# Merge gates of an encoder block as block products of seven, on one Trainium2 core

## The chip, the cores and the metric

The kernel runs on one core of a Trainium2 chip. TensorE (PE) does the matmuls and transposes, VectorE (DVE), ScalarE (ACT) and GpSimd (POOL) the elementwise work, and SyncE (SP) sends nearly all DMAs from one queue, in order. The metric is the device time of one execution in microseconds; less is better.

## The reference, cut to what matters

`x` is 1024 tokens by 1024 channels. All projections share one normalised input:

```python
h = rms_norm(x, g_pre[layer])
a_qkv, bq, bk, bv, mq, ga, gb, gm, mg = jnp.split(h @ w_in[layer], split_at, axis=-1)
...                       # oa: dilated window attention in 3 groups, with rotary positions
...                       # ob: grouped-query attention, om: cross-attention into a memory
ya = (oa * jax.nn.silu(ga)) @ w_br_a[layer]
yb = (ob * jax.nn.silu(gb)) @ w_br_b[layer]
ym = (om * jax.nn.silu(gm)) @ w_br_m[layer]
gates = jax.nn.sigmoid((mg + b_merge[layer]).astype(jnp.float32)).astype(dt).reshape(b, s, N_BRANCHES, d)
merged = gates[:, :, 0] * ya + gates[:, :, 1] * yb + gates[:, :, 2] * ym
out = merged @ w_out[layer]
x = x + rms_norm(out, g_post[layer])
```

`mg`, the pre-activation of the merge gates, is a 1024 x 1024 by 1024 x 3072 product. It is what the change computes in another way.

## The kernel before

Operands of the big products are split into a high and a low part (`split`: an ACT copy that rounds, then a DVE subtraction), and a product is made of three matmuls, high by high, high by low and low by high. Tokens stand as `hh[k]`, `hl[k]`, eight tiles of 128 channels x 1024 tokens each. A dense *unit* (`load_w`, `dense`) projects all tokens to 128 output channels: one 512 KB weight load, one split, and for each token half 8 channel tiles x 3 terms = 24 matmuls of 128x512, 48 in all. `mg` has 24 such units, numbered j = 8 i + f for branch i and output tile f.

The program runs in stages. Keys and values of the grouped-query attention and the memory projections come first, then cross-attention, then the grouped-query stage (`b_att`), then the dilated attention (pool `aa`, twelve items (p, g)), then the merge, then the output projection. In the attention stages `weave` interleaves dense units from a queue with the attention's own steps, in proportion to costs that are written in the code; PE's order is the order of recording throughout. A unit's result leaves PSUM by `evac`. `add_gate` makes SiLU gates and stores them to `g2d`; `add_filler` does a merge-gate unit early: times `rb` (the token's scale), tanh, stored to `thd`. `FILL_B = (13, 7, 6, 5, 4, 15, 14)` are filled into the grouped-query stage, beside nine SiLU gates, and `FILL_A = (3, 11, 12)` into the last dilated item.

In the grouped-query stage the steps are counted by n, one per key block. `row_max` is a matmul and a DVE minimum of 512 scores (into `bn`); after eight of them `bnm` is formed, `shift` transposes it and DVE writes it into `QL`; `scores` is two matmuls, the second of which reads `QL`, and an ACT exponential into `bp`; POOL adds the `bp` tiles into `bl`; `pv` is the value product, eight fp32 matmuls, and `final` a sum of `bl`. `LAG_S`, `LAG_T`, `LAG_P`, `LAG_F` (9, 10, 12, 13) say how many n each step trails.

In the merge, `mg_unit` computes one of the 14 units that are left (or loads a filled one), and `y_unit`, two units behind, makes a branch product: 24 matmuls of the gated branch output (`gh`, `gl`) with `w_br`, then DVE's (tanh + 1) times the product and a POOL addition into `accs[f]`. Outputs of the branches come back from `od`, gates from `g2d`, and for branch 1 reciprocal sums from `rld`. The order on ACT, DVE, POOL and SP is left to a scheduler here. Then `wout` is loaded and split, and eight token tiles are projected, normalised and stored.

Of the kernel before, what the change touches and what calls it, by code (L numbers as in the profile page):

```python
# [14 lines left out]
D = 1024  # L15
# [35 lines left out]
def block(ctx: ExitStack, tc: tile.TileContext, x, xT, memT, cst, msk, bcst, tabA, gpost,  # L51
# [179 lines left out]
    wgd = dram.tile([4, 2, 3, S], F32, name="wgd")  # L231

# [410 lines left out]
    with tc.tile_pool(name="ba", bufs=1, reuse_waits="tile") as ba:  # L643
# [31 lines left out]

        def b_att():
            st = {}

            def row_max(i, x):
# [6 lines left out]
                PE.matmul(s, QH[:, kv * 4 + j], KS[:, kv, c * 512:c * 512 + 512], start=True, stop=True)  # L686
                V.tensor_reduce(st[i]["n"][:, j, c:c + 1], s, axis=AX.X, op=OP.min)  # L687
                if x == 7:
                    V.tensor_tensor(nmt[i % 2][:, 64:68], st[i]["n"][:, :, 0], st[i]["n"][:, :, 1], op=OP.min)
# [107 lines left out]
    cbp, cb = pool("cb", "right")  # L797
    with tc.tile_pool(name="aa", bufs=1, reuse_waits="tile") as aa:
# [22 lines left out]
        def rope_half(o, half, p, scale, g):  # L821

            t = slice(half * 512, half * 512 + 512)
            t1 = aa.tile([P, 512], F32, name="t1a", bufs=3)
            t2 = aa.tile([P, 512], F32, name="t2a", bufs=3)
# [253 lines left out]
        def combine(p_, ogs):  # L1079
# [4 lines left out]
            def load(g):  # L1084
                wgt[g] = (aa if p_ < 3 else cb).tile([P, S], F32, name="wgt", bufs=3 if p_ < 3 else 1)
# [40 lines left out]

        todo = []
# [6 lines left out]
        for n in range(len(seq)):  # L1134
            if n + 2 < len(seq):
                add_a(*seq[n + 2])
            elif n + 2 == len(seq):
                for j in FILL_A:
                    add_filler(j)
            last = n + 1 == len(seq)  # L1140
            pieces = plan(items[n], items[n - 1] if n else None, items[n + 1])
            if last:
                pieces += plan(None, items[n], None)
            weave(len(FILL_A) if last else 3, run(pieces), sum(c for _, c in pieces), 1.0)

    end_psum()
# [3 lines left out]
    with tc.tile_pool(name="mg", bufs=1, reuse_waits="tile") as mg:  # L1150
        accs = [None] * 8
        extra.extend((mg, wp))

        def mg_unit(i, f):
            th = mg.tile([P, S], F32, name="th", bufs=3)
            if 8 * i + f in spilled:
                nc.sync.dma_start(th, thd[8 * i + f])
                return th
            w = load_w(wu[U_M + 8 * i + f])
            s = pss()  # L1160
            for half in range(2):
                for _ in dense(w, half, s[:, half]):
                    pass
            V.tensor_tensor(th, s.rearrange("p a b -> p (a b)"), rb, op=OP.mult)
            A.activation(th, th, AF.Tanh, scale=0.5, bias=hbm[:, 8 * i + f:8 * i + f + 1])
            return th

        def y_unit(n, i, f, th, gh, gl):
            wh, wl = load_w(wbr[i, f], 512)
            s = pss()  # L1170
            for half in range(2):
                t = slice(half * 512, half * 512 + 512)
                terms = []
                for k in range(4):
                    terms += [(wh[:, k, :], gh[k][:, t]), (wh[:, k, :], gl[k][:, t]), (wl[:, k, :], gh[k][:, t])]
                passes(s[:, half], terms)
            sv = s.rearrange("p a b -> p (a b)")
            if n == 0:
                accs[f] = mg.tile([P, S], F32, name=f"acc{f}")
                V.scalar_tensor_tensor(accs[f], th, 1.0, sv, op0=OP.add, op1=OP.mult)  # L1180
            else:
                V.scalar_tensor_tensor(th, th, 1.0, sv, op0=OP.add, op1=OP.mult)  # L1182
                G.tensor_tensor(accs[f], accs[f], th, op=OP.add)  # L1183

        def g_load(i):
            ots = []
            for k in range(4):
                ot = (pre or mg).tile([P, S], F32, name="ot", bufs=4 if pre else 2)
                nc.sync.dma_start(ot, od[i, k])
                gt = mg.tile([P, S], F32, name="gt", tag="wr", bufs=2)  # L1190
                nc.sync.dma_start(gt, g2d[i, k])
                V.scalar_tensor_tensor(ot, ot, 0.5, gt, op0=OP.mult, op1=OP.mult)
                if i == 1:
                    gt = mg.tile([P, S], F32, name="gt", tag="wr", bufs=2)
                    for h in range(2):
                        nc.sync.dma_start(gt[h * 64:h * 64 + 64], rld[2 * k + h:2 * k + h + 1].to_broadcast([64, S]))
                    V.tensor_tensor(ot, ot, gt, op=OP.mult)
                ots.append(ot)
            return ots

        def g_split(ots):
            gh, gl = [], []
            for k, ot in enumerate(ots):
                a = mg.tile([P, S], R, name=f"gh{k}")
                b = mg.tile([P, S], R, name=f"gl{k}")
                split(a, b, ot)
                gh.append(a)
                gl.append(b)
            return gh, gl

        def g_prep(i):
            gh, gl = [], []
            for k in range(4):
                ot = mg.tile([P, S], F32, name="ot", bufs=2)
                nc.sync.dma_start(ot, od[i, k])
                gt = mg.tile([P, S], F32, name="gt", tag="wr", bufs=2)
                nc.sync.dma_start(gt, g2d[i, k])
                V.scalar_tensor_tensor(ot, ot, 0.5, gt, op0=OP.mult, op1=OP.mult)
                a = mg.tile([P, S], R, name=f"gh{k}")
                b = mg.tile([P, S], R, name=f"gl{k}")  # L1220
                split(a, b, ot)
                gh.append(a)
                gl.append(b)
            return gh, gl

        pre = None
        steps = [(n, i, f) for n, i in enumerate((2, 1, 0)) for f in range(8)]
        ths = {}
        for m in range(len(steps) + 2):
            if m < len(steps):  # L1230
                n, i, f = steps[m]
                ths[m] = mg_unit(i, f)
            if m >= 2:
                n, i, f = steps[m - 2]
                if f == 0:
                    if n == 0:
                        gg = g_prep(i)
                        for step in combine(3, [OG.pop((3, x)) for x in range(3)]):
                            step()
                        close(cbp)  # L1240
                        prep, pre = pool("pre", "right")
                    else:
                        gg = g_split(ots)
                if f == G_AT and n < 2:
                    ots = g_load(1 - n)
                y_unit(n, i, f, ths.pop(m - 2), *gg)

        close(prep)
        fo = ctx.enter_context(tc.tile_pool(name="fo", bufs=1, side="right", reuse_waits="tile"))
        gp = fo.tile([P, D], F32, name="gp")  # L1250
        nc.sync.dma_start(gp, gpost)
        wo = []
        for k in range(8):
            raw = wp.tile([P, 1024], F32, name="wr", bufs=WR)
            nc.sync.dma_start(raw, wout[k])
            a = hp.tile([P, D], R, name=f"woh{k}", tag="big")
            b = hp.tile([P, D], R, name=f"wol{k}", tag="big")
            split(a, b, raw)
            wo.append((a, b))
        for T in range(NT):  # L1260
            t = slice(T * 128, T * 128 + 128)
            ah = wp.tile([P, 8, 128], R, name="wh")
            al = wp.tile([P, 8, 128], R, name="wl")
            for k in range(8):
                A.activation(ah[:, k], accs[k][:, t], AF.Copy, scale=0.5)
                V.scalar_tensor_tensor(al[:, k], accs[k][:, t], 0.5, ah[:, k].bitcast(F32), op0=OP.mult, op1=OP.subtract)
            sv = pss().rearrange("p a b -> p (a b)")
            cuts = [(0, 512), (512, 1024)] if T < NT - 1 else [(0, 512), (512, 768), (768, 1024)]
            terms = []
            for a, b in cuts:  # L1270
                c = slice(a, b)
                terms.append([])
                for k in range(8):
                    terms[-1] += [(ah[:, k], wo[k][0][:, c]), (ah[:, k], wo[k][1][:, c]), (al[:, k], wo[k][0][:, c])]
# [153 lines left out]
```

## Time and profile before

| what | value |
|---|---|
| median of 3 runs | 1502.12 us (1501.77 to 1502.21) |
| profiled execution, its own time | 1502.03 us |
| its span, first to last instruction | 1500.2 us |
| mean granted TensorE clock | 0.997 |
| PE idle in the span | 26.0 us (1500.2 - 1474.2) |
| grouped-query value products | first at 249.22 us, last at 553.85 us |
| DMA | 119.77 MB, 80 GB/s on average |

Busy times count an instruction from start to modelled end; matmuls overlap, so PE's pace is read from the number of matmuls in a window, not from the length of one. A line such as L687 names a line of the program as printed above. `<-` after the idle time names what ended it.

### The profile page before, as it was taken

To read this page: it belongs to the slowest core of one execution; us is meant where nothing else is said; L and a number is where in the kernel's file an instruction comes from. 1 tells how busy PE (TensorE), PEld (TensorE's weight loads), DVE (VectorE), ACT (ScalarE), POOL (GpSimd) and SP (SyncE) were. 2 spreads that over 40 slices of the span, in tenths; PEclk is the share of its full clock that TensorE was granted. 3 is DMA by queue.
4 is the path that set the end of the run, shared out by engine and by line. 5 is a ranking of instruction groups with operands and counts; after the bars stand their busy time and mean duration, and the time that the engine had idled before them with its cause. 6 is when DMAs were issued, how large, how long until landed. Compare 5 with 4: busy or idle time off the path is not lost.

```text
span 1500.2 us, 20621 instructions
## 1 busy us (share of the span) xinstructions
PE 1474.2 (98%) x7844; PEld 1185.7 (79%) x7844; DVE 838.9 (56%) x1514; ACT 576.4 (38%) x1307; POOL 444.7 (30%) x357
## 2 busy tenths in 40 slices
PE   7999989999999999999999999999999999999998
PEld 7899977667766668888888888888887888888787
DVE  7756466666555435664566567556526442525743
ACT  6543344444444341453444434343443112122321
POOL 1425413444444452321232223123200000223322
PEclk9999999999999999999999999999999999999999
DMA  6332011111211112111121121112136531623432
GB/s 241 103 99 71 30 49 60 56 61 43 64 57 50 56 60 89 43 30 43 45 72 57 43 73 44 43 44 72 57 102 189 176 99 43 216 64 113 137 102 99
DMA packets 55042, 119.77 MB, mean 80 GB/s; under 512 B 13792, under 2 KB 23712, under 8 KB 54816
## 3 DMA queue, kind: packets, MB, share of 16 engines
q1 hardware_dynamic: 54800, 118.34, 25.2%
q8 instruction: 61, 1.00, 0.3%
q14 instruction: 37, 0.30, 0.1%
q10 hardware_dynamic: 144, 0.13, 0.0%
HBM read 96.06 MB, written 22.38 MB: 79 GB/s over the span
## 4 chain that ended last, share of the span: by engine, by line
PE 88%; DVE 5%; DMA 2%; ACT 2%; issue 2%; POOL 1%; SPq 0%; POOLq 0%; DVEq 0%; ACTq 0%
PE d L143 14%; PE d L147 14%; PE d L145 14%; PE sc L125 7%; PE ov L720 4%; PE sc L1282 4%; PE sc L147 3%; PE sc L143 3%; PE sc L145 3%; PE tr L981 3%; PE s L918 2%; PE s L705 2%; PE s L704 2%; PE tr L686 2%; PE d L533 2%
## 5 line engine op out<-in xcount | busy, mean ns | idle before, releaser
L143 PE MATMUL d<-hh,wh 128*128 128x512 f32 x992 | 396.4, 400 | 1.8 <-DVE fth L222 1.8
L147 PE MATMUL d<-hh,wl 128*128 128x512 f32 x992 | 397.4, 401 | 0.0
L145 PE MATMUL d<-hl,wh 128*128 128x512 f32 x992 | 393.3, 397 | 0.0
L105 ACT ACTIVATE wh<-wr 128x1024 fp32r<-128x1024 f32 (+1 forms) x100 | 95.4, 955 | 354.9 <-PE d L145 162.7
L143 PEld LDWEIGHTS d<-hh,wh 128*128 128x128 f32 x992 | 187.1, 189 | 47.1 <-issue 5.0
L145 PEld LDWEIGHTS d<-hl,wh 128*128 128x128 f32 x992 | 186.9, 188 | 42.7 <-issue 5.7
L147 PEld LDWEIGHTS d<-hh,wl 128*128 128x128 f32 x992 | 187.0, 188 | 42.1 <-issue 4.7
L711 POOL TENSOR_TENSOR bl<-bl,bp 128x512 f32<-128x512 f32 x96 | 128.6, 1340 | 142.0 <-ACT bp L707 137.3
L106 DVE TENSOR_TENSOR wl<-wr,wh 128x1024 fp32r<-128x1024 f32 (+1 forms) x100 | 113.7, 1138 | 24.9 <-ACT wh L105 24.7
L687 DVE TENSOR_REDUCE bn<-tr 128x1 f32<-128x512 f32 x128 | 87.6, 689 | 63.6 <-PE tr L686 62.3
L707 ACT ACTIVATE bp<-s 128x512 f32<-128x512 f32 x128 | 75.3, 595 | 84.7 <-PE s L705 84.4
L1183 POOL TENSOR_TENSOR acc<-acc,th 128x1024 f32<-128x1024 f32 x16 | 45.4, 2839 | 202.5 <-DVE th L1182 202.5
L837 POOL TENSOR_TENSOR aq<-t1a,t2a 128x512 f32<-128x512 f32 x24 | 54.5, 2272 | 163.6 <-DVE t1a L831 157.5
L831 DVE SCALAR_TENSOR_TENSOR t2a<-d,tab 32x512 f32<-32x512 f32 x96 | 65.9, 687 | 62.7 <-PE d L147 57.8
L837 POOL TENSOR_TENSOR ak<-t1a,t2a 128x512 f32<-128x512 f32 x24 | 55.1, 2297 | 118.3 <-DVE t1a L830 118.3
L147 PE MATMUL sc<-hh,wl 128*128 128x512 f32 x224 | 87.3, 390 | 1.7 <-DVE wl L106 1.7
L143 PE MATMUL sc<-hh,wh 128*128 128x512 f32 x224 | 87.3, 390 | 0.0
L145 PE MATMUL sc<-hl,wh 128*128 128x512 f32 x224 | 87.2, 389 | 0.0
L830 DVE TENSOR_TENSOR t2a<-d,tab 32x512 f32<-32x512 f32 x96 | 65.9, 687 | 23.5 <-PE d L147 22.1
L930 DVE CUSTOM_DVE_ANT_0 pra<-s,mask 128x192 f32<-128x192 f32 (+2 forms) x192 | 56.7, 349 | 36.3 <-PE s L918 24.5
L125 PE MATMUL sc<-gh,wh 128*128 128x512 f32 x192 | 74.7, 389 | 0.0
L125 PE MATMUL sc<-gl,wh 128*128 128x512 f32 x192 | 74.7, 389 | 0.0
(263 smaller groups left out, 2716.4 us busy)
## 6 DMA issues: line engine op xcount, KB each, us to landing
wr<-in_wu SPq DMA_DIRECT2D x76, 512.0 KB
g2d<-fth SPq DMA_DIRECT2D x24, 256.0 KB
wgt<-wgd SPq DMA_DIRECT2D x24, 256.0 KB
ot<-od SPq DMA_DIRECT2D x12, 512.0 KB
gt<-g2d SPq DMA_DIRECT2D x12, 512.0 KB
wr<-in_wbr SPq DMA_DIRECT2D x24, 256.0 KB
thd<-fth SPq DMA_DIRECT2D x20, 256.0 KB
th<-thd SPq DMA_DIRECT2D x10, 512.0 KB
```

Source lines behind the costliest of these rows:

```text
L105: A.activation(dst_h, src, AF.Copy)
L106: V.tensor_tensor(dst_l, src, dst_h.bitcast(F32), op=OP.subtract)
L125: PE.matmul(out_ps, a, b, start=i == 0, stop=i == n - 1)
L143: PE.matmul(dst, wh[:, k, :], hh[k][:, t], start=k == 0, stop=False)
L145: PE.matmul(dst, wh[:, k, :], hl[k][:, t], start=False, stop=False)
L147: PE.matmul(dst, wl[:, k, :], hh[k][:, t], start=False, stop=k == 7)
L687: V.tensor_reduce(st[i]["n"][:, j, c:c + 1], s, axis=AX.X, op=OP.min)
L707: A.activation(pp, s, AF.Exp, scale=-1.0)
L711: G.tensor_tensor(lsum[i % 2], lsum[i % 2], pp, op=OP.add)
L830: return V.tensor_tensor(out, x, y, op=OP.mult)
L831: return V.scalar_tensor_tensor(out, x, scale, y, op0=OP.mult, op1=OP.mult)
L837: G.tensor_tensor(half_of(o, half, g), classes(t1, g), classes(t2, g), op=OP.add)
```

## The change

Two merge-gate units are taken as one pair. With the pair's weights cut into four blocks of 512 channels by 128 outputs (A11, A12 of the first unit, A21, A22 of the second) and the tokens into four blocks of 512 channels by 512 tokens (B11, B12, B21, B22), the four result blocks are made from seven block products instead of eight, by the Winograd form of Strassen's scheme. A block product is 4 channel tiles x 3 terms = 12 matmuls. Sums of weight blocks (S1 to S4) are made on POOL, for each pair; sums of token blocks (T1 to T4) once, on DVE in the grouped-query stage, split and stored to DRAM in `tsd`, and loaded again for the merge. T4 is loaded over the upper token half of `hh[0..3]`, `hl[0..3]`. Result sums are made on DVE from PSUM, and the tanh goes to `thd` for all units.

22 units become 11 pairs; two are still whole, as fillers of the grouped-query stage. Three SiLU gates move from that stage to the last dilated item. In the pairs and in the branch products that follow them, the queues of ACT, DVE, POOL and SP are in the order of recording (`manual_schedule`). Branch products run after all pairs; their gated operands are written over `hh` and `hl`; output weights are loaded and split during the last eight of them.

```diff
+    tsd = dram.tile([4, 4, 2, P, 512], F32, name="tsd")
...
+        def token_block(k):
+            tb = [ba.tile([P, 512], F32, name=f"tb{j}", bufs=1) for j in range(4)]
...
+            def store(j, src):
+                def fn():
+                    h = ba.tile([P, 512], R, name="tbh", bufs=2)
+                    l = ba.tile([P, 512], R, name="tbl", bufs=2)
+                    split(h, l, src)
+                    for x, part in enumerate((h, l)):
+                        nc.sync.dma_start(tsd[j, k, x], part.bitcast(F32))
+                return fn
+            b11, b12, b22, b21 = tb
+            return [whole(b12, k, 1), whole(b11, k, 0), sub(b11, b12, b11), store(0, b11),
+                    whole(b22, k + 4, 1), sub(b12, b22, b12), store(2, b12),
+                    sub(b22, b22, b11), store(1, b22), whole(b21, k + 4, 0), sub(b21, b21, b22), store(3, b21)]
...
                     row_max(i, x)
+                    if n in (14, 38, 62, 86):
+                        blocks += token_block((n - 14) // 24)
+                    if blocks and n % 2 == 0:
+                        with tc.issue_after(fp["last"].ins):
+                            blocks.pop(0)()
                     yield 216
...
-                if (i, p_) not in ((2, 0), (2, 1), (2, 2)):
+                if (i, p_) not in ((2, 0), (2, 1), (2, 2)) + GATES_A:
...
-                for j in FILL_A:
-                    add_filler(j)
+                for j in GATES_A:
+                    add_gate(*j)
+                early[len(queue)] = first_blocks
...
+                load_block("T2")
+                load_block("T3")
...
+    manual = tc.manual_schedule(engines={ET.Activation, ET.DVE, ET.Pool, ET.SP})
...
+    PRODUCTS = (("A11", "B11"), ("A12", "B21"), ("S2", "T2"), ("S3", "T3"), ("A22", "T4"), ("S4", "B22"), ("S1", "T1"))
...
+    def prod(n, i):
+        an, bn = PRODUCTS[i]
+        dst = pss1()
+        ah, al = [v.rearrange("p (k f) -> p k f", k=4) for v in BL[n][an]]
+        passes(dst, [t for k in range(4) for t in (
+            (ah[:, k], TB[bn][k][0]), (ah[:, k], TB[bn][k][1]), (al[:, k], TB[bn][k][0]))])
+        return dst
...
+    def gate_out(n, u, t, x, z):
+        r = sr.tile([P, 512], F32, name="rs", bufs=2)
+        j = pairs[n][u]
+        add(r, x, z)
+        V.tensor_tensor(r, r, rb[:, half[t]], op=OP.mult)
+        return lambda: (A.activation(r, r, AF.Tanh, scale=0.5, bias=hbm[:, j:j + 1]),
+                        nc.sync.dma_start(thd[j, :, half[t]], r))
...
+    load_block("T3", (2, 3))
+    for j in (1, 2, 3, 4):
+        weight_sum(0, j)
+    load_block("T4")
+    load_pair(1, 0)
+    load_pair(1, 1)
+    load_block("T1")
+    before = None
+    for n in range(len(pairs)):
+        for i in range(7):
+            ps_ = prod(n, i)
+            then = evac(*before) if before else None
+            slot(n, i)
+            if then:
+                then()
+            before = (n, i, ps_)
+    evac(*before)()
...
+    th_load(0)
+    yp = None
+    for m, (n, i, f) in enumerate(steps):
+        s = y_unit(m)
+        if yp:
+            y_evac(*yp)
+        yp = m, s
+        th_load(m + 1)
+        y_load(m + 2)
+        y_split(m + 1)
+        if n < 2:
+            j = 1 - n
+            for what, at in ((g_split, 2), (g_mult, 1), (g_load, 0)):
+                if f - at in (0, 1, 3, 4):
+                    what(j, (0, 1, 0, 2, 3)[f - at], *([slice(0, S)] if at == 2 else []))
+            if j == 1 and f in (0, 1, 3, 4):
+                r_load((0, 1, 0, 2, 3)[f])
+        if m >= 15 and m < 23:
+            wo_load(m - 15)
+        if n == 2:
+            split(*wo[f], raws[f])
...
-START_PAD, END_PAD = 250, 300
+START_PAD, END_PAD = 700, 300
...
-FILL_B = (13, 7, 6, 5, 4, 15, 14)
-FILL_A = (3, 11, 12)
+FILL_B = (16, 17)
+GATES_A = ((0, 1), (0, 2), (0, 3))
```

`slot(n, i)` spreads the preparation over the seven products of a pair: the splits of A22, S4 and S1 in the first three, the next pair's sums and splits in the middle ones, its loads at i = 1 and, two pairs ahead, at i = 6, and the rest of the dilated attention's combination and the first gated operands where they fall due. `evac` handles the product before: P1 is copied by ACT; running sums `v`, `y`, `w` are kept on DVE; four blocks per pair go through `gate_out`. In the branch products, `g_load` fetches a branch output (`ot`) and its gate (`gt`), `r_load` the reciprocal sums (`rt`), `g_mult` multiplies them, `g_split` splits them into `hh` and `hl`; `gt` and `rt` have one buffer each.

More of the change, by code (lines that the diff above doesn't have):

```diff
@@ L1143, in block @@
                 pieces += plan(None, items[n], None)
-            weave(len(FILL_A) if last else 3, run(pieces), sum(c for _, c in pieces), 1.0)
+            weave(len(GATES_A) if last else 3, run(pieces), sum(c for _, c in pieces), 1.0)
+    end_psum()
+    phase_psum("ps_w", s1=6)
+    manual = tc.manual_schedule(engines={ET.Activation, ET.DVE, ET.Pool, ET.SP})
+    manual.__enter__()
+    lo, hi = half
+    srp, sr = pool("sr")
+    t1p, t1l = pool("t1")
+    SF = [sr.tile([P, 512], F32, name=f"sf{j}") for j in range(4)]
@@ new lines, in part, with weight_sum, block_of @@
+    def part(n, j):
+        return BL[n][j // 2][:, half[j % 2]]
+    def weight_sum(n, j):
+        u, v, op = {1: (part(n, 2), part(n, 3), OP.add), 2: (SF[0], part(n, 0), OP.subtract),
+                    3: (part(n, 0), part(n, 2), OP.subtract), 4: (part(n, 1), SF[1], OP.subtract)}[j]
+        G.tensor_tensor(SF[j - 1], u, v, op=op)
+    def block_of(n, nm):
+        src = part(n, 3) if nm == "A22" else SF[int(nm[1]) - 1]
+        t = sr.tile([P, 2, 512], R, name="ch", bufs=5)
+        split(t[:, 0], t[:, 1], src)
+        BL[n][nm] = t[:, 0], t[:, 1]
@@ new lines, in prod, with add @@
+    def prod(n, i):
[5 more added lines that the diff above has]
+        return dst
+    p1, v, y, w = [sr.tile([P, 512], F32, name=f"sp{j}") for j in range(4)]
+    def add(dst, x, z):
+        V.tensor_tensor(dst, x, z, op=OP.add)
+    def gate_out(n, u, t, x, z):
[5 more added lines that the diff above has]
+                        nc.sync.dma_start(thd[j, :, half[t]], r))
@@ new lines, in evac @@
+    def evac(n, i, ps_):
+        if i == 0:
+            A.activation(p1, ps_, AF.Copy)
+        elif i == 1:
+            return gate_out(n, 0, 0, ps_, p1)
+        elif i == 2:
+            add(v, ps_, p1)
+        elif i == 3:
+            add(y, ps_, v)
+        elif i == 4:
+            return gate_out(n, 1, 0, ps_, y)
+        elif i == 5:
+            add(w, ps_, v)
+        else:
+            outs = gate_out(n, 1, 1, ps_, y), gate_out(n, 0, 1, ps_, w)
+            return lambda: [f() for f in outs]
@@ new lines, in block, with th_load, wo_load @@
+    mgp, mg = pool("mg")
+    myp, my = pool("my")
+    accs = [None] * 8
+    wo = [(hh[k + 4], hl[k + 4]) for k in range(4)]
+    wo += [(mg.tile([P, D], R, name=f"woh{k}"), mg.tile([P, D], R, name=f"wol{k}")) for k in range(4, 8)]
+    raws, THS = {}, {}
+    def th_load(m):
+        if m < len(steps):
+            _, i, f = steps[m]
+            THS[m] = my.tile([P, S], F32, name="th", bufs=3)
+            nc.sync.dma_start(THS[m], thd[8 * i + f])
+    def wo_load(k):
+        raws[k] = my.tile([P, D], F32, name="raw", bufs=2)
+        nc.sync.dma_start(raws[k], wout[k])
@@ new lines, in y_unit, with y_evac @@
+    def y_unit(m):
+        n, i, f = steps[m]
+        wh, wl = YW.pop(m)
+        s = pss()
+        for h in half:
+            terms = []
+            for k in range(4):
+                gh, gl = [x[k + 4 * (i == 1)][:, h] for x in (hh, hl)]
+                terms += [(wh[:, k], gh), (wh[:, k], gl), (wl[:, k], gh)]
+            passes(s[:, int(h.start > 0)], terms)
+        return s
+    def y_evac(m, s):
+        n, i, f = steps[m]
+        sv = s.rearrange("p a b -> p (a b)")
+        th = THS.pop(m)
+        if n == 0:
+            accs[f] = mg.tile([P, S], F32, name=f"acc{f}")
+            V.scalar_tensor_tensor(accs[f], th, 1.0, sv, op0=OP.add, op1=OP.mult)
+        else:
+            V.scalar_tensor_tensor(th, th, 1.0, sv, op0=OP.add, op1=OP.mult)
+            G.tensor_tensor(accs[f], accs[f], th, op=OP.add)
```

333 lines of the change are left out of this document (183 added, 150 removed).

## The prediction

> **What bounds the kernel now.** I read the busy summary first, then the chain, then stage windows, then the groups of the grouped-query stage, then single places of the timeline.
>
> ```profile
> PE 1474.2 (98%) x7844; PEld 1185.7 (79%) x7844; DVE 838.9 (56%) x1514; ACT 576.4 (38%) x1307; POOL 444.7 (30%) x357
> PE 88%; DVE 5%; DMA 2%; ACT 2%; issue 2%; POOL 1%; SPq 0%; POOLq 0%; DVEq 0%; ACTq 0%
> ```
>
> PE is busy for all but 26 us of the 1500.2 us span, and the chain that ended last is PE for 88%. So a matmul removed is time removed, as long as PE is still fed. The windows (length, then busy us and count for PE, PEld, DVE, ACT, POOL, then clock, DMA share, GB/s) show the pace and the few holes:
>
> ```profile
> 0.00:20.00 20.00, 13.65 (x99) 13.36 (x100) 12.20 (x19) 14.64 (x21) 0.19 (x4) 1.00 0.93 328
> 210.00:220.00 10.00, 7.50 (x30) 6.12 (x31) 5.81 (x10) 3.07 (x9) 2.42 (x3) 0.66 0.16 54
> 1120.00:1130.00 10.00, 10.00 (x45) 8.26 (x45) 4.03 (x10) 3.29 (x5) 0.00 (x0) 1.00 0.84 286
> 1150.00:1160.00 10.00, 8.31 (x37) 6.56 (x35) 5.63 (x3) 2.73 (x3) 2.39 (x1) 1.00 0.49 133
> 1200.00:1300.00 100.00, 100.00 (x442) 82.79 (x442) 41.80 (x39) 21.10 (x23) 4.45 (x2) 1.00 0.36 109
> 1410.00:1420.00 10.00, 8.73 (x38) 6.57 (x37) 6.28 (x15) 5.23 (x14) 4.09 (x3) 1.00 0.19 56
> ```
>
> 1200 to 1300 is pure merge work: 442 matmuls in 100 us, 0.2263 us each, whatever the 0.39 us that one is drawn long. 1150 to 1160 loses 1.7 us at the start of the merge, 1410 to 1420 loses 1.3 us before the output projection. At 210 to 220 PE had gaps and then ran at a granted clock of 0.66. The groups of 240 to 540 us, the grouped-query stage (busy us and mean ns, then idle time before), and two lines of its timeline (start, length):
>
> ```profile
> L687 DVE TENSOR_REDUCE bn<-tr 128x1 f32<-128x512 f32 x115 | 79.2, 690 | 63.2 <-PE tr L686 62.0
> L106 DVE TENSOR_TENSOR wl<-wr,wh 128x1024 fp32r<-128x1024 f32 x14 | 18.8, 1340 | 0.6 <-ACT wh L105 0.5
> L689 DVE TENSOR_TENSOR bnm<-bn 128x4 f32<-128x4 f32 x15 | 7.7, 515 | 0.4
> L711 POOL TENSOR_TENSOR bl<-bl,bp 128x512 f32<-128x512 f32 x90 | 120.1, 1335 | 134.3 <-ACT bp L707 130.0 <-DVE fth L220 0.9
> 387.13 4.06 POOL L711 TENSOR_TENSOR bl<-bl,bp 128x512 f32<-128x512 f32 x3 [0.19 <-ACT bp L707]
> 387.83 0.61 DVE L689 TENSOR_TENSOR bnm<-bn 128x4 f32<-128x4 f32 x1
> ```
>
> bnm has four columns and takes 0.14 us at its shortest, 0.515 on average. The last two lines say why: it starts inside a POOL addition and ends at 388.44, where the first of POOL's three (1.30 us) ends. A DVE operation with both inputs in SBUF waits here for POOL, 0.37 us on average.
>
> **The matmuls.** Before, 24 merge-gate units of 48 matmuls: 1152. After, two whole units (96) and 11 pairs of 7 products of 12 (924): 1020. The instruction lists of the two built programs agree: 7204 and 7072 matmuls and transposes, 132 fewer. New and old are the same 128x512 form, so 132 x 0.2263 = **29.9 us off**. Nothing else on PE changes in number.
>
> **Steady merge.** Per pair PE needs 84 x 0.2263 = 19.0 us. DVE gets 11 additions and products and 5 splits of 512 columns (16 x 0.69) and one split of 1024 (1.22): 12.3 us; ACT one copy, four tanh, five and one splits, 0.6 + 4 x 0.72 + 5 x 0.63 + 1.06 = 7.7; POOL four sums of 1.34, 5.4. Everything fits under PE, and six banks let PE run up to six products ahead. I cost it at nothing; if DVE lost its cover, the excess over 19.0 would count eleven times. SP's loads go out two to four products ahead of use.
>
> **Moved units.** The grouped-query stage goes from 16 whole units to 8 (6 gates, 2 fillers); three gates take the place of three fillers in the last dilated item, an even trade but for one 0.69 us DVE product per half, under idle DVE. The 8 units' 87 us leave a stage where they were cover. Per group of 8 key blocks PE's list now holds 8 maxima, 16 score matmuls, 2 of the sum and some 22 dense, 48 x 0.2263, plus 3.58 for the value product: 14.5 us, against some 20.5 us between value products in the trace.
>
> **Token sums in that stage.** Forty-eight DVE operations (16 sums, 16 differences, 16 split remainders), four per group in twelve groups, all with two SBUF inputs, 16 ACT copies and 32 stores of 256 KB on SP. DVE per group before them: 8 maxima 5.5, QL 0.69, obt 0.68, bll 0.74, bnm 0.5, half a query preparation 0.69, dense evictions 1.85: 10.7 us. The new ones add 4 x 0.69 = 2.8, and 4 x 0.37 of waits for POOL: 15.0 in all, just over PE's 14.5. What PE waits for is QL: by the lists it has 15 matmuls and a transpose, 3.5 us, from a group's eighth maximum to the score that needs QL (4.4 where a query preparation lies between). DVE there has the maximum, a gate product or a further maximum, bnm, another maximum, one token operation and QL: 5 x 0.69 + 0.14 = 3.6, two waits of 0.37, and about 0.5 for the token operation that it is still in: 4.8. That is 1.3 us late without a query preparation, 0.4 with one, and some 0.2 more for the maxima queued behind it: **1.0 us per group, 12 us in all**. Bounds: with no wait for POOL 4 us; with half a POOL addition (0.67) at each of the three, 20, and if the whole DVE excess shows, 26. I take 12 since bnm's measured mean is the nearest row.
>
> **Start of the merge.** After the last value product SP sends the rest of T3 (1 MB), T4 (2 MB, over `hh` and `hl`), the next pair (1 MB) and T1 (2 MB): 6.29e6 bytes, behind the last gate's store. The two densest windows moved 286 and 328 GB/s; in the middle 20.5 us, with 2.5 us for issue and landing 23 us. The seventh product needs the last quarter of T1 at 6.75 x 2.72 = 18.4 us: **4.6 us late** (3.3 to 6.1). POOL's first sums and S2, S3 are made before this. PE's gaps there can lower the clock: after waits of 2.60 and 1.55 us around 210 us PE ran 6.5 us at 0.50, 3.2 us lost. The new gaps are split by T1's quarters, about 1.2 us each, so I take half, **1.5 us** (0 to 3.2). [...] The 1.7 us lost at 1150 us goes.
>
> **Start of the branch products.** `th_load(0)` stands on SP behind the last tanh store, 4 us into the first unit; then 2.75 MB follow until `rt` of the first tile is there, about 15.5 us. (In the trace `rld` loads issued at 1194.39 were waited for until 1199.25.) DVE takes `g_mult` in hand order ahead of the eviction and of the weight split that the fourth unit needs at 16.3 us: done at about 20, **4 us late** (0 if the loads run ahead, 8 if the single `gt` and `rt` buffers repeat it). Output weights are split during the last eight units, so the 1.3 us before the projection goes.
>
> **Sum** on the profiled run's own 1502.0 (span 1500.2 and 1.8 around it, 0.1 from the median): 1502.0 - 29.9 - 1.7 - 1.3 + 12 + 4.6 + 1.5 + 4 = **1491.2 us**. All low bounds give 1476.4 (4 + 3.3 + 0 + 0 added back), all high ones 1512.4 (26 + 6.1 + 3.2 + 8).
>
> **Rivals.**
> *The covers hold.* From 230 to 240 us DVE was busy 9.15 of 10 us while PE lost only 0.3; if token operations fall into the value products, where DVE has nothing to do, the low bounds apply: 1476.4 us. Against it: they are queued behind maxima, not in that gap. Chance 0.22.
> *POOL and DVE block each other in the grouped-query stage* and it ends slower. POOL's 9.4 us of additions per group must fit into a group of 14.5 us instead of 20.5, so a token operation meets one more often; it decides from 1.9 us per group, when 12 x 1.9 = 23 eats what is left. At a wait of 0.9 us instead of 0.37 at each of the three (wol, split beside POOL's `acc` additions, went from 1.2 to 3.4 us at worst), a group loses 2.5 us, 30 us: 1509 us. Against it: bll, in the same stage, mostly took its bare 0.69. Chance 0.22. [...]
> *The saving isn't delivered*: seven products with hand-ordered queues leave PE waiting for evictions, 2.5 us in each pair: 1502 + 27.5 - 32.9 + 5 = 1502. The 12.3 of 19.0 us speaks against it. Chance 0.06.
>
> **How the numbers follow.** The forecast case has 0.50 and spans 1480 to 1499. Low and high tails beyond 1474 and 1510 are about one in ten each. A measurement of this kernel can tell 0.2%, 3.0 us, from no change. Faster: the forecast but its upper edge, 0.48, and the first rival, 0.22, 0.70; within: 0.07; slower: 0.23.
>
> **What would show it.** Right: 132 fewer matmuls at 0.226 us; PE waits on QL's line of about 1 us per group in the twelve groups with token lines and not in the others; one wait on T1 in the first pair; a wait on a weight split early in the branch products. Wrong: DVE or POOL as the releaser through the pairs, waits on QL under 0.3 or over 2 us per group, or no PE wait at the start of either part.

## The result, and the profile after

The changed kernel takes 1516.29 us (median of 5 runs, 1511.99 to 1517.31), the kernel before beside it 1502.21 us: a ratio of 1.0082 (of the means, as all ratios below), 95% interval 1.0061 to 1.0103. It is slower by 0.8%, and lies above the whole range of the forecast. The profiled execution took 1515.56 us (span 1513.8). First its busy summary and the shares of the chain that ended last:

```profile
PE 1461.9 (97%) x7712; PEld 1164.2 (77%) x7712; DVE 990.3 (65%) x1701; ACT 614.0 (41%) x1396; POOL 521.0 (34%) x401
PE 72%; DVE 12%; DMA 5%; issue 4%; ACT 3%; POOL 3%; SPq 1%; DVEq 0%; POOLq 0%; ACTq 0%
```

PE has its 132 matmuls less, and idles for 51.9 us instead of 26.0; DVE, DMA, ACT and POOL now hold 23% of the chain, where they held 10%. The stretches that the forecast named (length, then busy us and count for PE, PEld, DVE, ACT, POOL, then clock, DMA share, GB/s):

```profile
1070.00:1080.00 10.00, 7.52 (x21) 5.49 (x22) 6.86 (x8) 3.73 (x6) 6.59 (x4) 0.66 0.70 243
1100.00:1120.00 20.00, 17.39 (x69) 13.58 (x68) 18.33 (x19) 7.15 (x11) 7.58 (x4) 0.91 0.49 144
...
1200.00:1250.00 50.00, 50.00 (x222) 41.42 (x221) 34.28 (x45) 18.55 (x29) 12.80 (x8) 1.00 0.51 171
1300.00:1310.00 10.00, 6.80 (x27) 4.71 (x27) 6.98 (x7) 3.04 (x4) 0.00 (x0) 1.00 1.01 315
1410.00:1420.00 10.00, 10.00 (x46) 8.29 (x45) 9.72 (x9) 3.63 (x9) 6.08 (x2) 1.00 0.41 134
```

Steady pairs are what was forecast: 222 matmuls in 50 us, PE without a gap, DVE busy for two thirds. The gap before the projection (1410 to 1420) is gone. The losses are at the start of the pairs, in the third pair and at the start of the branch products. The groups of 240 to 540 us, the grouped-query stage, on DVE and POOL:

```profile
L684 DVE TENSOR_TENSOR tb<-hh,hl 128x512 f32<-128x512 f32 x16 | 20.7, 1291 | 0.0
L106 DVE TENSOR_TENSOR tbl<-tb,tbh 128x512 fp32r<-128x512 f32 x16 | 17.0, 1063 | 0.1
L687 DVE TENSOR_TENSOR tb<-tb,tb 128x512 f32<-128x512 f32 x16 | 15.2, 947 | 0.2
...
L717 DVE TENSOR_TENSOR bnm<-bn 128x4 f32<-128x4 f32 x15 | 7.0, 465 | 0.3
...
L739 POOL TENSOR_TENSOR bl<-bl,bp 128x512 f32<-128x512 f32 x96 | 134.2, 1398 | 83.4 <-ACT bp L735 78.3
```

The 48 token operations last 1.10 us on average ((20.7 + 17.0 + 15.2) / 48), 0.41 over their bare 0.69: the wait for POOL that the forecast took from bnm (0.37). And what PE waited for in the stage (total, times, longest):

```profile
PE s L733 <- DVE QL L723: 7.6, 8, 1.8
PE tr L714 <- DVE bn L715: 4.0, 5, 0.9
PE tr L722 <- DVE bnm L717: 1.5, 3, 1.1
```

QL leads, then the maxima queued behind it. In the twelve groups with token operations, PE waited on QL for 1.20, 1.52, 0.22, 0.82, 1.76 and 1.52 us in the six without a query preparation, and not at all in the six with one.

These waits don't add up to what the stage loses. All PE waits there come to some 16 us; the half clock after the longest one (381.8 to 385.2) costs 1.7 more; and a part can't be seen as idle time at all, because the trace draws a dense matmul 0.39 us long where one starts each 0.2263, so a wait of up to 0.16 us behind it looks busy. Losses below are therefore taken from start times. The whole account, with 0.2263 us a matmul. The first dilated score started at 602.3 us before and at 537.5 after; with eight units (86.9 us) less it was due at 515.4, so the grouped-query stage loses **22.1 us**. The dilated stage takes 517.2 us, as it did. From the first pair's first matmul (1054.7) to the first branch matmul (1279.5) are 224.8 us where eleven pairs need 209.1: **15.7 lost**. From there to the projection (1420.0) 140.5 us where 24 products need 130.4: **10.1 lost**. (The wait of 2.5 us right before the first branch matmul is counted in the 15.7, though it belongs to the branch products. By pairs, the 15.7 are 7.2 in the first, 4.9 in the third, 0.7 in the fourth and 2.7 in the last, with that wait.) The merge before lost 2.6, and the projection is 1.9 shorter. -29.9 + 22.1 + 15.7 + 10.1 - 2.6 - 1.9 = +13.5; the spans differ by 13.6.

### The profile page after: what moved, and what is told of

It reads as the page before. It is cut to its first block, busy times and chain, and to the rows that moved or that the text cites. A ratio compares the mean times of both kernels' runs of the same rounds, so it can differ in the third digit from the quotient of the medians.

```text
span 1513.8 us, 21012 instructions
## 1 busy us (share of the span) xinstructions
PE 1461.9 (97%) x7712; PEld 1164.2 (77%) x7712; DVE 990.3 (65%) x1701; ACT 614.0 (41%) x1396; POOL 521.0 (34%) x401
## 4 chain that ended last, share of the span: by engine, by line
PE 72%; DVE 12%; DMA 5%; issue 4%; ACT 3%; POOL 3%; SPq 1%; DVEq 0%; POOLq 0%; ACTq 0%
PE d L143 12%; PE d L147 12%; PE d L145 12%; PE sc L125 7%; PE s L125 5%; PE sc L1499 4%; PE ov L748 4%; PE tr L1015 3%; DVE bn L715 2%; PE s L952 2%; DMA thd<-rs 2%; DVE tb L684 1%; DMA wr<-in_wbr 1%; POOL sf L1243 1%; PE s L733 1%
## 5 line engine op out<-in xcount | busy, mean ns | idle before, releaser
L143 PE MATMUL d<-hh,wh 128*128 128x512 f32 x864 | 345.9, 400 | 1.8 <-DVE fth L222 1.8
L147 PE MATMUL d<-hh,wl 128*128 128x512 f32 x864 | 347.2, 402 | 0.1
L145 PE MATMUL d<-hl,wh 128*128 128x512 f32 x864 | 342.7, 397 | 0.0
L143 PEld LDWEIGHTS d<-hh,wh 128*128 128x128 f32 x864 | 163.0, 189 | 43.5 <-issue 8.2
L147 PEld LDWEIGHTS d<-hh,wl 128*128 128x128 f32 x864 | 162.9, 189 | 36.4 <-issue 5.3
L125 PE MATMUL sc<-hh,wh 128*128 128x512 f32 x384 | 121.9, 398 | 7.6 <-ACT wh L105 5.1
L106 DVE TENSOR_TENSOR wl<-wr,wh 128x1024 fp32r<-128x1024 f32 x65 | 84.6, 1303 | 31.6 <-ACT wh L105 31.5
L1243 POOL TENSOR_TENSOR sf<-wr 128x512 f32<-128x512 f32 x22 | 38.1, 1751 | 162.8 <-DMA wr<-in_wu 67.2
L125 PEld LDWEIGHTS sc<-hh,wh 128*128 128x128 f32 x384 | 73.4, 192 | 25.6 <-ACT wh L105 6.2
L1001 ACT ACTIVATE app<-tr 128x384 f32<-128x384 f32 (+2 forms) x96 | 45.9, 478 | 71.5 <-PE tr L998 46.2
```

Source lines behind the costliest of these rows:

```text
L106: V.tensor_tensor(dst_l, src, dst_h.bitcast(F32), op=OP.subtract)
L125: PE.matmul(out_ps, a, b, start=i == 0, stop=i == n - 1)
L143: PE.matmul(dst, wh[:, k, :], hh[k][:, t], start=k == 0, stop=False)
L145: PE.matmul(dst, wh[:, k, :], hl[k][:, t], start=False, stop=False)
L147: PE.matmul(dst, wl[:, k, :], hh[k][:, t], start=False, stop=k == 7)
```

## The experiments

Six kernels ask what the grouped-query stage loses its time to. The number to compare is the stage's loss: the start of the first dilated score less 515.4 us.

**no_token**

```diff
-                    split(h, l, src)
-                    for x, part in enumerate((h, l)):
-                        nc.sync.dma_start(tsd[j, k, x], part.bitcast(F32))
+                    for x, part in enumerate((hh, hl)):
+                        nc.sync.dma_start(tsd[j, k, x], part[k][:, half[j % 2]].bitcast(F32))
...
-            return [whole(b12, k, 1), whole(b11, k, 0), sub(b11, b12, b11), store(0, b11),
+            return [lambda: None, lambda: None, lambda: None, store(0, b11), lambda: None, lambda: None, store(2, b12),
...
```

> Leaves out the arithmetic of the token sums: the 48 DVE operations and 16 ACT copies in the grouped-query stage are gone, the 32 stores stay and send the parts of the normalized tokens as they are (so the products S2..S1 get wrong operands). Theory A, the time lost in the grouped-query stage (22 us) is what the token operations do to the DVE: first dilated score at 515 to 518 us instead of 537.6, total 1494 to 1497. Rival B, it is the cover of the eight units that went, whatever the DVE does: the stage stays at 535 or later, total 1513 to 1517.

Measured: 1500.99 us, ratio to before 0.9976 (0.9966 to 0.9985). The stage loses 7.1 us instead of 22.1. So 15.0 us are the token operations, and 7.1 are not: neither theory alone. A row of this kernel that changed besides is bnm's:

```profile
L713 DVE TENSOR_TENSOR bnm<-bn 128x4 f32<-128x4 f32 x15 | 15.1, 1003 | 0.3
```

1.003 us where it took 0.515 before and 0.14 at its shortest. With most of POOL's additions left out it takes 0.153 (no_rowsum, below), so it seems to meet them more often here, or for longer. (In the changed kernel it takes 0.465; there the waits fall on the token operations first.) One place shows what a late maximum can cost: PE waits 1.98 us for one, until 321.7 us, and the half clock after that (322.5 to 325.9) costs 1.7 more. These 3.7 us are half of the 7.1. That bnm makes the other half isn't shown: waits on QL are 1.5 us in all here.

**no_rowsum**

```diff
-                elif kt > 1:
-                    G.tensor_tensor(lsum[i % 2], lsum[i % 2], pp, op=OP.add)
...
+        V.tensor_scalar(rl, rl, 1e-3, None, op0=OP.max)
         V.reciprocal(rl, rl)
```

> Leaves out POOL's row sums from the third key block on (12 of its 14 additions per two groups), so that POOL hardly works beside the DVE; all token sums stay. Theory A, the waits for POOL (0.41 us a token operation) are what turns a full DVE into a late one: token operations at 0.69, 0.41 x 4 x 12 = 20 us back, total 1496 to 1500. Rival B, the number of operations is the cause and the waits are hidden: total 1511 to 1516.

Measured: 1498.98 us, ratio 0.9963 (0.9949 to 0.9978); the stage loses 3.6 us, with all token operations where they were. Their lines:

```profile
L687 DVE TENSOR_TENSOR tb<-tb,tb 128x512 f32<-128x512 f32 x16 | 11.0, 687 | 0.2
L106 DVE TENSOR_TENSOR tbl<-tb,tbh 128x512 fp32r<-128x512 f32 x16 | 10.9, 684 | 0.1
L684 DVE TENSOR_TENSOR tb<-hh,hl 128x512 f32<-128x512 f32 x16 | 10.9, 682 | 0.0
L717 DVE TENSOR_TENSOR bnm<-bn 128x4 f32<-128x4 f32 x15 | 2.3, 153 | 0.0
```

All at their bare length; 18.5 us come back, bnm's waits included. Theory A: without the waits for POOL the same DVE work nearly fits. The maxima, which read PSUM, show no such wait: they take 0.684 us with POOL's additions (the changed kernel) and 0.685 without.

**token_places**

```diff
-                    if blocks and n % 2 == 0:
+                    if blocks and n % 8 in (2, 3, 4, 5):
```

> All work stays. The token operations go behind maxima 2, 3, 4 and 5 of a group instead of 0, 2, 4 and 6, so none stands between a group's eighth maximum and its shift (QL). Theory A, the loss is QL being late by the token operation ahead of it (the step of the prediction): waits on QL (7.6 us) gone and 8 to 14 us back, total 1502 to 1508. Rival B, the DVE's whole work per group is what counts: the waits move to the maxima, total within 3 us of 1516.

Measured: 1500.93 us, ratio 0.9978 (0.9967 to 0.999), just under what A expected; the stage loses 7.4 us, as if the token operations were not there. The DVE does the same work and still meets POOL (0.94 to 1.09 us for sums and differences), though less: the split remainders take 0.76 us instead of 1.06, and the 48 operations 0.93 on average instead of 1.10. Whether that or the place gives the 14.7 us is settled by the next two kernels.

**token_x0** and **token_x6** move one of the four operations each.

```diff
-                    if blocks and n % 2 == 0:
+                    if blocks and n % 8 in (2, 3, 4, 6):      # token_x0
+                    if blocks and n % 8 in (0, 2, 3, 4):      # token_x6
```

> All work stays; only one of the four token operations of a group moves: behind maxima 2, 3, 4, 6 instead of 0, 2, 4, 6 (none behind a group's eighth maximum any more). Theory A, as the prediction counted it, it is this one that makes QL late: most of the 15 us that token_places gave come back, total 1502 to 1506. Rival B, the one behind maximum 6, which delays the eighth maximum itself, weighs as much: half comes back, 1507 to 1511.

> The counterpart of token_x0: behind maxima 0, 2, 3, 4 instead of 0, 2, 4, 6, so that only the operation ahead of the eighth maximum moves. Theory A: little comes back, total 1512 to 1517. Rival B: half comes back, 1507 to 1511.

Measured: 1503.52 us (ratio 1.0, 0.9987 to 1.0013) and 1516.22 us (1.0083, 1.0062 to 1.0104); the stage loses 8.6 and 20.2 us. Nearly everything hangs on the operation behind maximum 0. It is the place that counts, and not how much of POOL the operations meet in all: in token_x0 the 48 still take 1.00 us on average, 0.31 over their bare length, and 13.5 of the 22.1 us are back. The DVE's timeline of a group in the changed kernel (start, length; the eighth maximum is the one ahead of bnm) and of one in token_x0:

```profile
427.25 1.49 DVE L106 TENSOR_TENSOR tbl<-tb,tbh 128x512 fp32r<-128x512 f32 x1
428.66 0.68 DVE L715 TENSOR_REDUCE bn<-tr 128x1 f32<-128x512 f32 x1
429.37 0.54 DVE L717 TENSOR_TENSOR bnm<-bn 128x4 f32<-128x4 f32 x1
429.83 0.68 DVE L715 TENSOR_REDUCE bn<-tr 128x1 f32<-128x512 f32 x1
430.44 1.35 DVE L684 TENSOR_TENSOR tb<-hh,hl 128x512 f32<-128x512 f32 x1
431.72 0.68 DVE L715 TENSOR_REDUCE bn<-tr 128x1 f32<-128x512 f32 x1
432.42 0.69 DVE L723 TENSOR_TENSOR QL<-tr,cs 4x512 fp32r<-4x512 f32 x1
```

```profile
415.07 1.50 DVE L106 TENSOR_TENSOR tbl<-tb,tbh 128x512 fp32r<-128x512 f32 x1
416.49 0.68 DVE L715 TENSOR_REDUCE bn<-tr 128x1 f32<-128x512 f32 x1
417.20 0.54 DVE L717 TENSOR_TENSOR bnm<-bn 128x4 f32<-128x4 f32 x1
417.67 1.27 DVE L715 TENSOR_REDUCE bn<-tr 128x1 f32<-128x512 f32 x2
418.97 0.69 DVE L723 TENSOR_TENSOR QL<-tr,cs 4x512 fp32r<-4x512 f32 x1
```

The split ahead of the eighth maximum is equally long in both. From the start of the eighth maximum to that of QL are 3.76 us and 2.48: the 1.28 between them is the token sum, lengthened by POOL. Rival B falls.

**lags**

```diff
-LAG_S, LAG_T, LAG_P, LAG_F = 9, 10, 12, 13
+LAG_S, LAG_T, LAG_P, LAG_F = 9, 11, 13, 14
```

> All work stays. Scores, value products and row sums run one key block later behind the maxima (lags 11, 13, 14 instead of 10, 12, 13), so QL has some 1.0 us more. Theory A, QL's latency: its waits gone, 7 to 12 us back, total 1504 to 1509. Rival B, the DVE's whole work per group: waits on the maxima take their place, total within 3 us of 1516.

Measured: 1506.41 us, ratio 1.0017 (1.0006 to 1.0029), as A expected; the stage loses 12.2 us. Waits on QL no longer show, 2.6 us of waits on maxima are left. More distance between QL and its reader serves the same end, less well than moving the operation.

Four more take token_places and change the merge. What to compare is the loss of the pairs (15.2 us in token_places) and of the branch products (11.2).

**first_pair**

```diff
                 weight_sum(n + 1, 1)
                 weight_sum(n + 1, 3)
-                own_blocks(n + 1)
+                if n:
+                    own_blocks(n + 1)
             elif i == 4:
+                if first:
+                    own_blocks(1)
                 weight_sum(n + 1, 2)
```

> As token_places, and in the first pair the split of the next pair's own weights goes behind the split of S4 in the hand order of ACT and DVE. Theory A, the 7 us lost in the first pair are this order (ACT's copy waits for a weight load, S4 behind it): the waits on ch of 2.2 and 1.2 us and the half clock after them go, 4 to 7 us less than token_places: 1494 to 1497. Rival B, the step of the prediction (T1's load is late by 4.6 us): the wait turns into one on the load of T1, at most 2 us less: 1499 to 1502.

The trace of the changed kernel had shown why (start, length, the wait before):

```profile
1069.65 1.06 ACT L105 ACTIVATE wh<-wr 128x1024 fp32r<-128x1024 f32 x1 [6.51 <-DMA wr<-in_wu]
1070.61 0.61 ACT L105 ACTIVATE ch<-sf 128x512 fp32r<-128x512 f32 x1
1070.73 1.23 DVE L106 TENSOR_TENSOR wl<-wr,wh 128x1024 fp32r<-128x1024 f32 x1 [6.29 <-ACT wh L105]
1071.28 0.79 PE L125 MATMUL s<-hh,ch 128*128 128x512 f32 x1 [2.17 <-ACT ch L105]
1072.48 1.16 DVE L106 TENSOR_TENSOR ch<-sf,ch 128x512 fp32r<-128x512 f32 x1
1073.70 1.22 PE L125 MATMUL s<-hh,ch 128*128 128x512 f32 x2 [1.20 <-DVE ch L106]
```

ACT and DVE stand still for over 6 us behind a weight that only the next pair needs, and S4's split, which PE wants now, is queued behind it. Measured: 1498.64 us (ratio 0.997, 0.9957 to 0.9982), between the two expected ranges, and its interval overlaps that of token_places. In the trace, of the slowest of its ten runs (1501.96 us), the pairs lose 15.3 us as before. The first pair's two waits on S4 and its half clock are gone, as theory A says, but it still loses 5.1 us instead of 6.7: the product with T4 takes 2.3 us longer than PE needs and that with T1 2.7, both waiting for their loads, as rival B says. And new waits stand in the pairs after it:

```profile
1097.67 0.73 PE L125 MATMUL s<-hh,ch 128*128 128x512 f32 x2 [1.80 <-DVE ch L106]
1107.12 0.50 PE L125 MATMUL s<-hh,wl 128*128 128x512 f32 x1 [1.00 <-DVE wl L106]
```

So both theories hold in part: the loads and the DVE's next trouble were hidden by the wait on S4.

**mix_spread**

```diff
-    COM = {(0, 0): 0, (1, 0): 1, (1, 3): 2, (1, 6): 3, (2, 2): 4}
+    COM = {(0, 0): 0, (1, 1): 1, (1, 6): 2, (2, 6): 3, (3, 6): 4}
...
-        if (n, i) == (3, 0):
+        if (n, i) == (4, 0):
```

> As token_places, and the three products of the last dilated combination (2 to 3 us of DVE each) go into slot 6 of pairs 1, 2 and 3 instead of slots 3 and 6 of pair 1 and 2 of pair 2. Theory A, the 4.9 us lost in the third pair come from them standing ahead of weight splits on the DVE: waits on ch around the third pair gone, 4 to 5 us less than token_places: 1496 to 1497. Rival B, the clock is lowered by something else there: 1499 to 1502.

Measured: 1492.38 us, ratio 0.9931 (0.9906 to 0.9956), 4 us better than expected. The pairs lose 8.4 us instead of 15.2, the branch products 9.1. No wait is left from the second pair to the last: the third and fourth lost 4.3 and 0.7 us in token_places and lose nothing here, which is what theory A expected. The rest of the gain is not in these pairs: the wait of 3.0 us right before the first branch product has gone too, for a reason that these runs don't show, and the first pair loses 1.2 us more.

**branch_order**

```diff
-            if i == 0:
+            if i == 1:
                 y_load(0)
                 y_load(1)
...
-            if i == 2:
+            if i == 4:
                 y_split(0)
+            elif i == 2:
+                g_side(0)        # gt and rt of the first group
+            elif i == 6:
+                g_main(0)        # its ot
...
-        th_load(m + 1)
         y_load(m + 2)
+        th_load(m + 1)
         y_split(m + 1)
-        if n < 2:
+        if n == 0:
+            if f in (0, 2, 4, 6):
+                g_mult(1, f // 2)
+            if f in (1, 3, 5, 6):
+                g_split(1, f // 2, slice(0, S))
+            if f in (0, 2, 4):
+                g_side(f // 2 + 1)
+                g_main(f // 2 + 1)
+        if n == 1:
```

> As token_places, and the start of the branch products is reordered: the first two branch weights are loaded behind the tanh stores of the pair before, the gate, row sum and attention rows of the first group are loaded in the last pair, and those of the next three groups every second unit, each with its product two units later. Theory A, the 12.7 us lost there are SP's order and single buffers: waits on hh and wh gone, 8 to 11 us less than token_places: 1490 to 1493. Rival B, the DMA engines are full there (298 GB/s) whatever the order: 1497 to 1502, with waits on wh as before.

What it was to mend, in the changed kernel's timeline:

```profile
1262.73 4.01 SPq L1323 DMA_DIRECT2D wr<-in_wbr  x2
1270.03 0.69 DVE L1262 TENSOR_TENSOR rs<-s,sp 128x512 f32<-128x512 f32 x1 [1.72 <-DMA thd<-rs]
...
1300.12 0.63 ACT L105 ACTIVATE wh<-wr 128x512 fp32r<-128x512 f32 x1 [8.06 <-DMA wr<-in_wbr]
1300.80 0.50 PE L125 MATMUL sc<-hh,wh 128*128 128x512 f32 x1 [2.67 <-ACT wh L105]
```

Two branch weights hold SP for 4.01 us, 3.2 of them a wait for a free buffer; the tanh stores stand behind them, the DVE waits for one of them before it may write `rs`, and the gated operands that PE needs next are split late. Later the branch weights stand behind loads into `gt` and `rt`. Measured: 1493.93 us, ratio 0.9935 (0.9918 to 0.9952). The branch products lose 5.7 us instead of 11.2, and PE still waits 4.4 us there. Closer to A; a part stays, and no run separates DMA bandwidth from order in it.

**all_three** is first_pair, mix_spread and branch_order together.

> token_places with the three changes of first_pair, mix_spread and branch_order together. If the losses are separate places as read from the trace: 16 to 23 us less than token_places, 1478 to 1485, and so faster than the kernel before by 1.2 to 1.6%. If the merge is short of DVE or DMA time as a whole, a loss taken from one place comes back at the next: 1490 or more.

Measured: 1484.09 us, ratio 0.9873 (0.9858 to 0.9887). Pairs lose 4.3 us, branch products 5.0. All PE waits from the first pair to the projection:

```profile
PE sc L125 <- ACT wh L105: 1.9, 2, 1.7
PE s L125 <- DMA T<-tsd: 0.7, 3, 0.3
PE sc L125 <- ACT hh L105: 0.3, 1, 0.3
PE s L125 <- DMA hl<-tsd: 0.2, 1, 0.2
```

Here first_pair's edit pays: with mix_spread alone the pairs lost 8.4. Of the 4.3 us left, 3.5 are in the first pair, and 2.8 of these in the product with T1, although the list has only 0.7 us of waits on `T`. Its twelve matmuls and the next pair's first:

```profile
1056.71 0.40 PE L125 MATMUL s<-T,ch 128*128 128x512 f32 x1
1057.26 1.17 PE L125 MATMUL s<-T,ch 128*128 128x512 f32 x3
1058.62 1.18 PE L125 MATMUL s<-T,ch 128*128 128x512 f32 x3 [0.18 <-DMA T<-tsd]
1060.09 1.37 PE L125 MATMUL s<-T,ch 128*128 128x512 f32 x3 [0.29 <-DMA T<-tsd]
1061.64 0.73 PE L125 MATMUL s<-T,ch 128*128 128x512 f32 x2 [0.18 <-DMA T<-tsd]
1062.22 0.39 PE L125 MATMUL s<-hh,wh 128*128 128x512 f32 x1
```

They take 5.5 us where 2.7 is due, at a clock of 1.00.

**all_fill4** and **all_lags**, on top of all_three:

```diff
-FILL_B = (16, 17)
+FILL_B = (16, 17, 18, 19)                               # all_fill4
-LAG_S, LAG_T, LAG_P, LAG_F = 9, 10, 12, 13
+LAG_S, LAG_T, LAG_P, LAG_F = 9, 11, 13, 14              # all_lags
```

> As all_three, with two more whole units in the grouped-query stage (fillers 16 to 19) and ten pairs instead of eleven: 12 more matmuls, 2.7 us. Theory A, some 7 us that the stage still loses without token work are cover that the eight moved units gave: 3 to 5 us of it come back, total 1482 to 1484. Rival B, that loss has nothing to do with cover: 1486 to 1488.

> As all_three, with scores, value products and row sums one key block later behind the maxima (lags 11, 13, 14). Theory A, what the grouped-query stage still loses is QL's latency (2.9 us of waits): 2 to 4 us less, 1480 to 1482. Rival B, the token operations then fall on other places and the DVE gets full again, as in lags, whose stage lost 12 us: 1485 to 1490.

Measured: 1488.53 us (ratio 0.9899, 0.9877 to 0.992) and 1482.87 us (0.9864, 0.9846 to 0.9882). Two more units of cover bring the stage's loss from 7.1 to 5.4 us, where theory A expected 3 to 5 us back and the extra matmuls cost 2.7: nearer to rival B. The ten pairs lost 9.9 us, with one wait of 5.6 on `rs` ahead of the branch products; there the DVE is busy without a gap from 1249.6 to 1260.3 us, with splits of gated operands between the last pair's evictions, but why this kernel alone waits there isn't shown. The longer lags take 2.3 us off the stage (4.8 lost), as theory A says, though the total lies just above its range; it is the lowest of these kernels, 1.4% under the kernel before, though its interval overlaps that of all_three.

## Why the prediction was wrong

The forecast for the profiled run was 1491.2 us, its time 1515.6: 24.4 us. By the account above the stage was worse by 22.1 - 12 = 10.1, the pairs by 15.7 - 6.1 = 9.6, the branch products by 10.1 - 4 = 6.1; the gains at the merge's start and before the projection were 1.5 us larger than taken. (With the wait before the first branch matmul counted where it belongs, the pairs were worse by some 7 and the branch products by some 8.6.)

**Right.** The matmuls: 132 fewer, and steady pairs at 19.0 us with DVE at two thirds; the rival of undelivered savings is out. The mechanism of the stage: QL late by a token operation between the eighth maximum and the score, one operation of the four (token_x0 against token_x6). The working had it 1.3 us late without a query preparation and 0.4 with one; PE waited 0.2 to 1.8 us in the groups without, and nothing in those with one. The wait for POOL was 0.41 us on average where 0.37 was taken; for the twelve operations in the place that counts it was 0.57 (1.26 us against 0.69).

**The token sums, 12 us.** They cost 15.0 by no_token, 14.7 by token_places, over the forecast's figure and far inside its bounds of 4 and 26. The working's "eighth maximum to QL" of 4.8 us was 4.45 in the group shown (3.76 + 0.69).

**The step that failed in this stage** is "Moved units", costed at no more than the cover that the 14.5 us per group gave: the stage loses 7.1 us without any token arithmetic. The wait of bnm for POOL was taken over from the old stage at 0.37 us; in no_token it was 0.86 (1.003 - 0.14). But token_places loses as much, 7.4 us, with bnm at 0.643, so bnm alone doesn't explain it. Without POOL's additions 3.6 us are lost, token operations included, so some half of the 7.1 hangs on POOL, and in no_token half is the one wait of 1.98 us on a maximum and the half clock after it; the rest has no shown cause. The longer `START_PAD` of the change, which spaces the stage's first steps, was not tested by itself. The rival "POOL and DVE block each other" priced the new operations' waits at 0.9 us; they were 0.41 to 0.57, but the stage came out near the point from which that rival decides (22.1 us against 23).

**Start of the merge, 4.6 us for T1 and 1.5 for the clock.** The place was right, and the cause wrong in the changed kernel. What PE waited for there was S4's split behind a weight of the next pair in hand order (2.17 and 1.20 us), and the half clock with it (0.50 from 1071.3 to 1078.1): 7.2 us in this pair, none of it on T1. The forecast read the loads' order on SP and did not follow ACT's own order past the waits. T1's lateness is real, but it was hidden behind S4: where S4's order is mended, T1's product loses 2.7 us (first_pair) and 2.8 (all_three), under the 3.3 that the range began with. The loads were faster than the sum took: 410 GB/s in the five us from 1065, against some 307. The trace of the kernel before had shown that speed: the 20 us window whose mean of 328 was read holds 181, 319, 402 and 410 in its four quarters. The 2.5 us for issue and landing in that sum were an estimate that no row shows by itself; in the kernel before, the DVE waited for a 512 KB load of `gt` until 3.34 us after its issue (1178.08 to 1181.42), transfer included.

**The third pair** was costed at nothing ("Steady merge"): the sum of DVE's work there left out the combination of the last dilated head, recorded into pairs 1 and 2, at 2.0 us a product, and 3.1 for the one beside POOL's weight sums (1099.3). The third pair loses 4.9 us and the fourth 0.7; mix_spread gives the two pairs' loss back. This term was missing, not mis-sized.

**Start of the branch products, 4 us.** The upper bound of 8 named the single `gt` and `rt` buffers, and they did repeat it: two waits of 2.67 and 2.40 us on branch weights behind their loads. The wait at the very start (2.5 us) was not in the sum: SP's branch weight ahead of the tanh stores.

The merge's terms went wrong in one direction for one reason. Each engine's work was added up and compared with PE's time, and where it fitted the cost was nothing. Where the queues are ordered by hand, an operation that waits holds up all that stand behind it, however idle its engine is: ACT stood 6.51 us at the head of its queue in the first pair.

## What to carry to other kernels

When a queue is in hand order, read it as a chain: for each operation ask what it waits for and who stands behind it, above all where a load for later stands ahead of work for now. Put extra work of a shared engine away from the step that another engine's next instruction reads; the same four operations cost some 15 us in one place and next to nothing in another. Losses in a row hide each other: with the wait on S4 mended alone, the first pair still lost 5.1 us of 6.7, to loads that had stood in its shadow, and the pairs as a whole lost as much as before in that trace; with all three mended, pairs and branch products together lose 17.1 us less. And compare windows of one length: a mean over a stretch that starts idle hides what a queue can move (328 GB/s against 410).

## What the runs showed of the hardware

The clock fell after short waits. In the changed kernel it was 0.50 from 1071.3 us, behind the wait of 2.17 us, and a second wait of 1.20 fell into that stretch (length, PE to POOL, clock, DMA share, GB/s):

```profile
1072.00:1074.00 2.00, 0.80 (x3) 0.31 (x2) 1.64 (x2) 0.00 (x0) 2.00 (x2) 0.50 1.06 388
...
1076.00:1078.00 2.00, 2.00 (x6) 1.61 (x5) 1.97 (x3) 0.63 (x1) 1.63 (x2) 0.50 0.22 76
1078.00:1080.00 2.00, 2.00 (x10) 1.55 (x10) 1.45 (x3) 1.25 (x2) 0.00 (x0) 0.97 0.06 23
```

Six matmuls in 2 us instead of some nine, until 1078.1. Five more drops to 0.50 stand in this trace ahead of its end: from 211.1 to 218.0, 381.8 to 385.2, 1115.7 to 1119.1, 1279.5 to 1282.9 and 1310.2 to 1313.6 us. The waits that ended nearest to their starts lasted 2.60, 1.76, 2.13, 2.54 and 2.40 us. Yet a wait of 2.67 us that ended at 1300.8 left the clock at 1.00 (1300 to 1310), and in first_pair so did the single wait of 1.80 us. So the length of the wait alone doesn't tell whether the clock falls: 1.76 us were enough once, and 2.67 were not. What decides there these runs don't show.

Loads of the token sums moved 410 GB/s over five us (1065 to 1070). The kernel before reached the same from 15 to 20 us.
